# Weight sums of the first two column pairs of the first MLP product: added by transfers from GpSimd's queue in place of VectorE

## The chip, the core and the metric

The kernel runs on one core of a Trainium2 chip. The core has a matrix engine (TensorE, PE in the profile), VectorE (DVE), ScalarE (ACT), GpSimd (POOL) and SyncE (SP), each with an in-order queue of its own, and 16 DMA engines that move data between DRAM and the core's memory. SP, ScalarE and GpSimd issue transfers; those that add into their destination are issued from GpSimd in this kernel. The metric is the time of one execution in device microseconds (us); lower is better.

## What is computed

One layer of an encoder on a 1024 x 1024 input in float32: a normalisation, mLSTM heads and differential attention side by side, an output projection, and an MLP. The change touches the MLP alone:

```python
u = rms(x, norm2_g[l]).astype(dt) @ w_ff1[l]     # 1024 x 1024 by 1024 x 4096
u = jnp.square(jax.nn.relu(u))
x = x + (u @ w_ff2[l]).astype(dt)
```

## The kernel before

Every float32 matrix product is made from three matmuls: each operand is cut into a high part (`cut_hi`, a copy on ScalarE) and the low rest (`cut_lo`, a subtraction on VectorE), and high x high, high x low and low x high are added up.

**The first MLP product.** The 4096 columns of the weight are 32 tiles of 128 columns, taken in 16 pairs, c = 0 to 15. Of a pair, tile 2c is loaded into `raw_e[c]` and tile 2c+1 into `raw_o[c]`, each 128 partitions x 2 halves x 512. Call the halves e0, e1 and o0, o1: the upper and lower 512 rows of the weight. The input is likewise split into four quarters, by rows and by tokens. Each pair is then computed with seven block products in place of eight, in the manner of Strassen and Winograd. Each block product is a `product` of 12 matmuls (four steps of k, three matmuls each), and is numbered:

| product | weight operand | tile that holds its parts | right operand |
|---|---|---|---|
| 1 | e0 | `w_a(c)`, half 0 | `x1` |
| 2 | e1 | `w_a(c)`, half 1 | `x2` |
| 6 | e0 + o0 + o1 ("u") | `wb`, half 0 | `x6` |
| 5 | o0 + o1 (`sum_s`, half 1 of "e") | `we`, half 1 | `x5` |
| 7 | o0 + e0 (`sum_7`, half 0 of "e") | `we`, half 0 | `x7` |
| 3 | e1 + e0 + o0 + o1 ("3") | `wb`, half 1 | `x3` |
| 4 | o1 ("d") | `wd0` or `wd1` | `x4` |

In the trace the parts carry an h or l (`weh`, `wel`). The weight sums are made in place, by VectorE, in this order: "d" is cut from o1 first, since the next sum overwrites o1; `sum_s` turns o1 into o0 + o1; `sum_7` turns o0 into o0 + e0; `sum_u` turns e0 into e0 + o0 + o1; `sum_3` turns e1 into e1 + e0 + o0 + o1. Then "u", "e" and "3" are cut. "e" is cut in one operation over both halves of `raw_o`.

**What sets the order.** Products 1 and 2 of the first six pairs run first, while the right operands are still being made; their results go to DRAM and are read back later. For that, e0 and e1 of pairs 0 and 1 are loaded once for the first products and a second time (`load_e(c, True)`, tiles `re0b` and `re1b`) for the sums. Then come the other five products pair by pair: 6, 5, 7, 3, 4 of pair 0, the same of pair 1, and so on.

The order on every queue is written out by hand: `when(t, f, ...)` puts a piece of work into a table at a time t, counted in block products, and the table is issued in order of t. The times set only the order; what an engine really waits for are its operands. The dictionary `moved` shifts single entries. In these units the last of the first products runs at 11; products 6, 5, 7, 3 and 4 of pair 0 stand at 12 to 16, and those of pair 1 at 17 to 21. Around them:

- `load_e` (line 1808) and `load_o` (1815) are issued by SP. `raw_o` of pair 1 goes into a slot that is free when the first `x5l` has been made.
- Lines 2014, 2017, 2020 and 2023 are the four sums.
- The cuts are lines 1789 (ScalarE) and 1792 (VectorE).
- `diff` (2080) makes the sums of quarters of the input, `make_v`, `make_w`, `c22`, `c12` and `c21` (1955 to 1970) combine results, and `relu2` (1925 to 1928) squares and stores them.
- GpSimd has nothing in its queue between 613 us (the root of the second normalisation) and the adding transfers for the weights of the second MLP product, from 733 us on.

Of the kernel before, what the change touches and what calls it, by code (L numbers as in the profile page):

```python
# [13 lines left out]
ALU = mybir.AluOpType  # L14
# [8 lines left out]
HB = 512  # L23
# [117 lines left out]
def hybrid_block_kernel(ctx: ExitStack, tc: tile.TileContext, xT, xR, w_v, w_k, w_c, w_va, w_qg, w_o, w_1, w_2, w_2q, vec, rel, outT):  # L141
    nc = tc.nc
# [176 lines left out]
    with tc.tile_pool(reuse_waits="tile", name="ps0", bufs=1, space=PSUM) as ps0:  # L319
# [219 lines left out]
        for i in range(2):  # L539
            n, k = [f"n{2 * i}", f"n{2 * i + 1}"], [f"kr{2 * i}", f"kr{2 * i + 1}"]  # L540
# [212 lines left out]
    clock, table, made = [0.0], [], []  # L753

    def when(t, f, *args):
        heapq.heappush(table, (t + moved.get(len(made), 0.0), len(made), f, args))
        made.append(t)
# [986 lines left out]
    for n in range(KT):  # L1744
        t = A["HF"] + u * parts_at[n][0][0]
# [3 lines left out]
        t = A["HF"] + u * ends[n]  # L1749
# [38 lines left out]
    def cut_hi(dst, src, idx=slice(None)):  # L1788
        nc.scalar.activation(dst[0][idx], src, AF.Copy)  # L1789

    def cut_lo(dst, src, idx=slice(None)):
        nc.vector.tensor_tensor(dst[1][idx], src, dst[0][idx].bitcast(F32), op=ALU.subtract)  # L1792
# [11 lines left out]
    raw_e, raw_o = {}, {}  # L1804

    def load_e(c, again=False):
        raw_e[c] = mpool2.tile([P, 2, HB], F32, tag="re", name=f"re{c}{'b' if again else ''}", bufs=2)
        nc.sync.dma_start(raw_e[c].rearrange("p a b -> p (a b)"), w_1[2 * c])

    def load_o(c):  # L1810
        if c % 2 == 0:
            raw_o[c] = mpool2.tile([P, 2, HB], F32, tag="ro", name=f"ro{c}")
        else:
            raw_o[c] = ypool.tile([P, 2, HB], F32, tag="y0_0", name=f"ro{c}")
        nc.sync.dma_start(raw_o[c].rearrange("p a b -> p (a b)"), w_1[2 * c + 1])
# [21 lines left out]
    for j in range(4):  # L1837
        t = A["XN"] + j * A["XD"]
# [3 lines left out]
        t = A["WN"] + j * A["WD"]  # L1842
# [19 lines left out]
    table = []  # L1862
# [36 lines left out]
    for c in range(N_FIRST):  # L1899
        when(max(2 * c - 1, 0), ops[1], c)  # L1900
        ends_at[1, c] = max(2 * c, 1)
        t = min(2 * c + 2, 2 * N_FIRST - 1)
        when(t, ops[2], c)
        ends_at[2, c] = t + 1
    t = 2 * N_FIRST
# [79 lines left out]
    for c in range(N_PAIR):  # L1985
        e = {i: ends_at[i, c] + 0.01 for i in ops}
# [12 lines left out]
        d = c == N_PAIR - 1  # L1999
# [11 lines left out]


    def sum_s(c):
        nc.vector.tensor_tensor(raw_o[c][:, 1], raw_o[c][:, 0], raw_o[c][:, 1], op=add)

    def sum_7(c):
        nc.vector.tensor_tensor(raw_o[c][:, 0], raw_o[c][:, 0], raw_e[c][:, 0], op=add)

    def sum_u(c):
        nc.vector.tensor_tensor(raw_e[c][:, 0], raw_e[c][:, 0], raw_o[c][:, 1], op=add)  # L2020

    def sum_3(c):
        nc.vector.tensor_tensor(raw_e[c][:, 1], raw_e[c][:, 1], raw_e[c][:, 0], op=add)

    parts_of = {
# [7 lines left out]
    def when_cut(hi, lo, x, c):  # L2033
        when(hi, lambda: cut_hi(*parts_of[x](c)))
        when(lo, lambda: cut_lo(*parts_of[x](c)))
# [4 lines left out]
    for n in range(1, N_PAIR):  # L2040
        b = begin[n - 1]
        if n == 1:

            when_cut(b + 2.2, b + 2.5, "d", n)
            when(b + 2.5, sum_s, n)
            when(b + 2.6, sum_7, n)
            when(b + 3.1, sum_u, n)
            when_cut(b + 3.45, b + 4.3, "u", n)
            when(b + 4.4, sum_3, n)
            when_cut(b + 3.8, b + 5.35, "e", n)  # L2050
            when_cut(b + 5.4, b + 5.9, "3", n)
        elif n <= N_FIRST:
            when_cut(b + 0.9, b + 1.55, "d", n)
            when(b + 1.6, sum_s, n)
            when(b + 2.3, sum_7, n)
            when(b + 2.31, sum_u, n)
            when_cut(b + 2.55, b + 2.8, "u", n)
            when(b + 3.3, sum_3, n)
            when_cut(b + 2.9, b + 3.55, "e", n)
            when_cut(b + 4.02, b + 4.25, "3", n)  # L2060
        else:
            when_cut(b + 2.5, b + 3.3, "d", n)
            when(b + 3.35, sum_s, n)
            when(b + 4.3, sum_7, n)
            when(b + 4.35, sum_u, n)
            when(b + 4.4, sum_3, n)
            when_cut(b + 5.3, b + 5.6, "e", n)
            when_cut(b + 5.8, b + 6.2, "u", n)
            when_cut(b + 7.5, b + 8.1, "3", n)
        if n >= N_FIRST:  # L2070
            when_cut(b + 1.5, b + 2.1, "a", n)
        if n + 2 < N_PAIR:
            when(begin[n] + (0.95 if n == 1 else -0.4 if n <= N_FIRST else 1.2), load_e, n + 2, n + 2 < N_FIRST)
            when(begin[n] + (0.95 if n == 1 else -0.8), load_o, n + 2)
# [10 lines left out]
    for j, t in enumerate((2.4, 3.6, 4.1, 4.6)):  # L2085
        when(t, normed, 1, j)
    when(0.1, load_e, 4)
    when(0.2, load_o, 0)
    when_cut(3.0, 3.2, "a", 4)
    when(3.1, load_e, 5)  # L2090
# [8 lines left out]
    for j in range(2):  # L2099
        d = 0.45 * j  # L2100
# [11 lines left out]
    when(10.2, sum_7, 0)  # L2112
    when(10.3, sum_u, 0)
    when_cut(10.5, 10.9, "u", 0)
    when_cut(10.95, 11.8, "e", 0)
    when(12.3, sum_3, 0)
    when_cut(12.4, 12.7, "3", 0)
    when(12.2, load_o, 1)
    when(12.5, load_o, 2)
    when(13.2, load_e, 2, True)  # L2120

# [13 lines left out]
    step_at, t = [], T2  # L2135
# [26 lines left out]
        table.append(x)  # L2162

    copier[0] = nc.sync

    def pairs(first, each, what):
        for n, (copy, more) in enumerate(zip(*what)):
            for x, d in ((copy, -2.6), (more, 0)):
                table.append((first + each * n + d, 10**6 + len(table), x[0], x[1:]))
# [209 lines left out]
    for s, (i, p, x) in enumerate(steps):  # L2379
        t, e = step_at[s], step_at[s + 1]  # L2380
        b = step_at[s - 2] if s >= 2 else T2 - 1.65 + 0.8 * s
# [19 lines left out]
        if p and x == 1:  # L2401
# [5 lines left out]
            if p in (2, 6, 3, 4):  # L2407
# [3 lines left out]
                else:  # L2411
                    d, one = {2: (r00, True), 3: (r01, True), 4: (zv, False)}[i]
# [127 lines left out]
```

## Time and profile before

| | |
|---|---|
| time, median of three runs | 1216.43 us (1215.98 to 1216.46) |
| the profiled execution: its own time / its span | 1220.52 / 1218.7 us |
| granted clock of TensorE | 1.00 |
| TensorE busy | 1205.9 us |
| VectorE / ScalarE / GpSimd busy | 909.6 / 705.3 / 307.6 us |
| bytes moved, mean rate | 276.85 MB, 227 GB/s |
| the first MLP product | from 607 us |
| products 6, 5, 7, 3, 4 of pair 0 | from 641.77 us |
| products 6, 5, 7, 3, 4 of pair 1 | from 656.90 us |

How to read the rows: a row of the order of time has its start and its duration in us, the engine, the line of the kernel, the operation, destination <- sources, and in brackets the idle time before it with what ended it. A row of waits has the total, the number of waits and the longest. A row of a window has its length, the busy time of TensorE, its weight loads, VectorE, ScalarE and GpSimd (with their instructions), the granted clock, the mean busy share of the 16 DMA engines, and GB/s. DMA rows give the size and the median time from issue to landing. Matmuls overlap, so their durations (0.39) are longer than the distance of their starts.

### The profile page before, as it was taken

The numbers are of one execution on the slowest core, as the hardware profiler recorded it, in microseconds if no ns is written. First come the engines' busy times: TensorE is split into PE (matmuls) and PEld (weight loads), VectorE is DVE, ScalarE is ACT, GpSimd is POOL, SyncE is SP. The second block draws the span as 40 slices with busy tenths as digits, with TensorE's granted clock in tenths as the row PEclk, the third lists the DMA queues.
The fourth block names the chain that finished last, engine by engine and source line by source line (L and its number), as shares of the span: only waits on it lengthen the run. The fifth ranks groups of instructions, "written<-read, shape, count | busy, mean of one in ns | idle before, by whom it ended". The sixth has DMA issues, their size and how long they took to land.

```text
span 1218.7 us, 18707 instructions
## 1 busy us (share of the span) xinstructions
PE 1205.9 (99%) x6925; PEld 1038.0 (85%) x6925; DVE 909.6 (75%) x1274; ACT 705.3 (58%) x1213; POOL 307.6 (25%) x359
## 2 busy tenths in 40 slices
PE   9999999999999999999999999999999999999998
PEld 8889888888878888888887788888888999999997
DVE  7885578984276787773889886666657878888888
ACT  7685457676456686654465454444536556555553
POOL 1135323553354474432400001010101102012111
PEclk9999999999999999999999999999999999999999
DMA  9972565344476799827955769989889979979896
GB/s 283 225 259 106 197 146 134 95 145 142 128 243 197 248 312 273 267 90 265 247 171 178 241 235 254 289 251 287 247 281 318 317 261 278 318 194 310 209 262 183
DMA packets 121919, 276.85 MB, mean 227 GB/s; under 512 B 11360, under 2 KB 36704, under 8 KB 121312
## 3 DMA queue, kind: packets, MB, share of 16 engines
q1 hardware_dynamic: 84980, 181.64, 44.5%
q0 software_dynamic: 24896, 72.39, 26.7%
q10 hardware_dynamic: 11952, 21.63, 4.8%
q8 instruction: 54, 0.88, 0.3%
q14 instruction: 37, 0.30, 0.1%
HBM read 216.28 MB, written 91.85 MB: 253 GB/s over the span
## 4 chain that ended last, share of the span: by engine, by line
PE 78%; DMA 9%; DVE 6%; ACT 3%; issue 2%; POOL 1%; SPq 0%; ACTq 0%; DVEq 0%; POOLq 0%
PE m L1876 7%; PE m L1878 7%; PE m L1877 7%; PE pav L1460 4%; PE pva L1330 4%; PE z L2289 4%; PE pl L1420 4%; PE z L2288 4%; PE z L2287 4%; PE z L2270 3%; PE z L2268 3%; PE z L2269 3%; PE pw L263 3%; PE pw L265 2%; PE pw L264 2%
## 5 line engine op out<-in xcount | busy, mean ns | idle before, releaser
L184 POOL DMA_DIRECT2D s<-in_w_dram x32 | 27.0, 843 | 261.1 <-DMA s<-s 194.2
L1425 DVE CUSTOM_DVE_ANT_0 l<-pl,toe 128x1024 f32<-128x1024 f32 x64 | 76.3, 1221 | 16.8 <-PE pl L1420 15.8
L1925 ACT ACTIVATE sq<-sq 128x512 f32<-128x512 f32 x48 | 30.2, 630 | 83.4 <-DVE sq L1964 64.2
L1431 ACT ACTIVATE l<-l,sm 128x1024 f32<-128x1024 f32 x64 | 73.2, 1148 | 0.5 <-DVE sm L1425 0.5
L2231 POOL DMA_DIRECT2D zw<-in_w_2q_dram x24 | 22.7, 1042 | 192.4 <-DVE wa1l L1792 40.5
L1460 PEld LDWEIGHTS pav<-v,at 128*128 128x128 f32 x512 | 61.5, 191 | 3.4 <-issue 1.1
L1460 PE MATMUL pav<-v,at 128*128 128x128 f32 x512 | 62.7, 275 | 0.0
L2289 PE MATMUL z<-wbh,wa1l 128*128 128x256 f32 x208 | 59.1, 284 | 0.6 <-DVE wa1l L1792 0.5
L2288 PE MATMUL z<-wbl,wa1h 128*128 128x256 f32 x208 | 58.9, 283 | 0.0
L2287 PE MATMUL z<-wbh,wa1h 128*128 128x256 f32 x208 | 58.8, 283 | 0.0
L1420 PE MATMUL pl<-kk,q 64*128 64x512 f32 x384 | 54.8, 409 | 0.2 <-DVE sm L1425 0.2
L263 PE MATMUL pj_c<-hhi,w_c 128*128 128x512 f32 x128 | 53.4, 417 | 0.0
L263 PE MATMUL pw<-mix,hi_wo 128*128 128x512 f32 x128 | 52.0, 406 | 0.0
L265 PE MATMUL pj_c<-hhi,w_c 128*128 128x512 f32 x128 | 50.2, 392 | 0.0
L265 PE MATMUL pw<-mix,lo_wo 128*128 128x512 f32 x128 | 50.0, 391 | 0.0
L264 PE MATMUL pj_c<-hlo,w_c 128*128 128x512 f32 x128 | 50.0, 390 | 0.0
L264 PE MATMUL pw<-mix,hi_wo 128*128 128x512 f32 x128 | 49.9, 390 | 0.0
L2270 PE MATMUL z<-weh,wa0l 128*128 128x512 f32 x120 | 46.9, 391 | 1.5 <-DVE wa0l L1792 1.5
L2268 PE MATMUL z<-weh,wa0h 128*128 128x512 f32 x120 | 47.0, 391 | 0.7 <-ACT wa0h L1789 0.7
L2269 PE MATMUL z<-wel,wa0h 128*128 128x512 f32 x120 | 46.9, 391 | 0.0
L1420 PEld LDWEIGHTS pl<-kk,q 64*128 64x128 f32 x384 | 34.9, 184 | 12.2 <-issue 4.6
L1465 ACT ACTIVATE on<-pav 128x128 f32<-128x128 f32 x32 | 8.9, 277 | 60.5 <-PE pav L1460 60.5
(549 smaller groups left out, 4195.6 us busy)
## 6 DMA issues: line engine op xcount, KB each, us to landing
s<-in_w_dram POOLq DMA_DIRECT2D x40, 512.0 KB, 7.8
g_dram<-gs SPq DMA_DIRECT2D x64, 256.0 KB, 5.7
zw<-s SPq DMA_DIRECT2D x32, 512.0 KB, 9.9
g<-g_dram SPq DMA_DIRECT2D x24, 512.0 KB, 9.4
zw<-in_w_2q_dram SPq DMA_DIRECT2D x24, 512.0 KB, 6.6
zw<-in_w_2q_dram POOLq DMA_DIRECT2D x24, 512.0 KB, 9.3
wide<-g_dram SPq DMA_DIRECT2D x24, 512.0 KB, 12.3
g_dram<-sq ACTq DMA_DIRECT2D x42, 256.0 KB, 4.2
```

The lines of the kernel that those rows point to most:

```text
L263: nc.tensor.matmul(out, ahi, bhi, start=start, stop=False)
L264: nc.tensor.matmul(out, ahi, blo, start=False, stop=False)
L265: latest[0] = nc.tensor.matmul(out, alo, bhi, start=False, stop=stop).ins
L1420: nc.tensor.matmul(it.pl[x][:, sl], hd.q[r, i, qi * P : (qi + 1) * P], hd.kk[r, j, sl], start=n == 0, stop=n == 2)
L1460: nc.tensor.matmul(it.pav[:, 0:P], at, it.head.v[:, c], start=c == 0, stop=c == NC - 1)
L1876: nc.tensor.matmul(p, wh, xh, start=go, stop=False, skip_group_check=True)
L1877: nc.tensor.matmul(p, wh, xl, start=False, stop=False, skip_group_check=True)
L1878: nc.tensor.matmul(p, wl, xh, start=False, stop=stop and k == 3, skip_group_check=True)
L2268: nc.tensor.matmul(p, wh, gh, start=go, stop=False, skip_group_check=True)
L2287: nc.tensor.matmul(o, wh[:, j, nn], gh[:, j], start=go, stop=False, skip_group_check=True)
L2288: nc.tensor.matmul(o, wh[:, j, nn], gl[:, j], start=False, stop=False, skip_group_check=True)
L2289: nc.tensor.matmul(o, wl[:, j, nn], gh[:, j], start=False, stop=end, skip_group_check=True)
```

## The change

For pairs 0 and 1 the four sums are not made by VectorE. Each operand is made in place by transfers that read a half of a weight tile from DRAM and add it to a half of `raw_e` or `raw_o` in the core's memory: 256 KB each, issued by GpSimd. `sum_s` and `sum_7` become one such transfer each, at the places where the sums stood; `sum_u` and `sum_3` issue nothing; in their place stand five transfers a pair into `raw_e`, which add o0 and o1 to e0, and e0, o0 and o1 to e1. These have times of their own in the table. Three cuts or loads get other times: "d" of pair 1 earlier, "e" of pair 0 later, `load_o` of pair 1 a little earlier. Pairs 2 to 15 are as before.

```diff
+    def add_block(raw, c, half, n):
+        nc.gpsimd.dma_start(raw[c][:, half], w_1[2 * c + n // 2][:, n % 2 * HB : (n % 2 + 1) * HB], accum_op=ALU.add)
...
     def sum_s(c):
+        if c < 2:
+            return add_block(raw_o, c, 1, 2)
         nc.vector.tensor_tensor(raw_o[c][:, 1], raw_o[c][:, 0], raw_o[c][:, 1], op=add)
 
     def sum_7(c):
+        if c < 2:
+            return add_block(raw_o, c, 0, 0)
         nc.vector.tensor_tensor(raw_o[c][:, 0], raw_o[c][:, 0], raw_e[c][:, 0], op=add)
 
     def sum_u(c):
+        if c < 2:
+            return None
         nc.vector.tensor_tensor(raw_e[c][:, 0], raw_e[c][:, 0], raw_o[c][:, 1], op=add)
 
     def sum_3(c):
+        if c < 2:
+            return None
         nc.vector.tensor_tensor(raw_e[c][:, 1], raw_e[c][:, 1], raw_e[c][:, 0], op=add)
...
-            when_cut(b + 2.2, b + 2.5, "d", n)
+            when_cut(b + 1.9, b + 2.1, "d", n)
...
-    when_cut(10.95, 11.8, "e", 0)
+    when_cut(12.0, 12.3, "e", 0)
...
-    when(12.2, load_o, 1)
+    when(11.95, load_o, 1)
...
     copier[0] = nc.sync
+    for t, c, adds in ((5.3, 0, ((0, 2), (1, 0))), (6.9, 0, ((0, 3), (1, 2))), (9.0, 0, ((1, 3),)), (9.01, 1, ((0, 2), (1, 0))),
+                       (10.9, 1, ((0, 3), (1, 2))), (12.2, 1, ((1, 3),))):
+        for half, n in adds:
+            table.append((t, 10**6 + len(table), add_block, (raw_e, c, half, n)))
```

In `add_block` n counts the four blocks of a pair: 0 and 1 are e0 and e1, 2 and 3 are o0 and o1.

## The prediction

> **What bounds the kernel now.** First the page's line of engines, then what TensorE waited for around the change, then TensorE's own order of time there.
>
> ```profile
> span 1218.7 us, 18707 instructions
> PE 1205.9 (99%) x6925; PEld 1038.0 (85%) x6925; DVE 909.6 (75%) x1274; ACT 705.3 (58%) x1213; POOL 307.6 (25%) x359
> ```
>
> TensorE is the bound: 99% of the span. Anything taken off another engine can give back only what TensorE waits for it. The waits of TensorE between 600 and 700 us:
>
> ```profile
> PE m L1876 <- ACT wbh L1789: 0.6, 1, 0.6
> PE m L1877 <- DVE x4l L1792: 0.4, 1, 0.4
> PE m L1876 <- DVE sq L1964: 0.3, 1, 0.3
> PE m L1876 <- DVE w L1959: 0.2, 1, 0.2
> ```
>
> Each is a wait of a few tenths, 1.5 us in all. Now TensorE itself: the first matmuls of products 6 and 5 of pair 0, the one of product 5 that first reads the low part `wel`, the two late ones, and the first matmul of product 5 of pair 1.
>
> ```profile
> 641.77 0.39 PE L1876 MATMUL m<-x6h,wbh 128*128 128x512 f32 x1
> 644.49 0.39 PE L1876 MATMUL m<-x5h,weh 128*128 128x512 f32 x1
> 644.95 0.39 PE L1878 MATMUL m<-x5h,wel 128*128 128x512 f32 x1
> ...
> 654.86 0.50 PE L1877 MATMUL m<-x4l,wd0h 128*128 128x512 f32 x1 [0.44 <-DVE x4l L1792]
> 656.90 0.50 PE L1876 MATMUL m<-x6h,wbh 128*128 128x512 f32 x1 [0.62 <-ACT wbh L1789]
> 660.02 0.39 PE L1876 MATMUL m<-x5h,weh 128*128 128x512 f32 x1
> ```
>
> A product of 12 matmuls takes 644.49 - 641.77 = 2.72 us, 0.227 a matmul. From 641.77 to 660.02 lie six products, which would take 16.33; they took 18.25. So 1.92 us is all that this stretch can give. With the later waits of 0.3 and 0.2 it is 2.4: about 0.2% of 1216.43, which is also about what a measurement of this kernel can tell from no change. Gain is capped; loss is not.
>
> **The change, part by part.** VectorE around it, and ScalarE's high part of `we`:
>
> ```profile
> 635.25 0.68 DVE L1792 TENSOR_TENSOR wd0l<-ro,wd0h 128x512 fp32r<-128x512 f32 x1
> 635.96 0.69 DVE L2014 TENSOR_TENSOR ro<-ro 128x512 f32<-128x512 f32 x1
> 636.69 0.69 DVE L2017 TENSOR_TENSOR ro<-ro,re0b 128x512 f32<-128x512 f32 x1
> 637.42 0.69 DVE L2020 TENSOR_TENSOR re0b<-re0b,ro 128x512 f32<-128x512 f32 x1
> ...
> 640.90 1.22 DVE L1792 TENSOR_TENSOR x5l<-y,x5h 128x1024 fp32r<-128x1024 f32 x1
> 642.04 1.21 DVE L1792 TENSOR_TENSOR wel<-ro,weh 128x1024 fp32r<-128x1024 f32 x1
> 643.17 0.68 DVE L2023 TENSOR_TENSOR re0b<-re0b 128x512 f32<-128x512 f32 x1
> 643.78 2.35 DVE L1792 TENSOR_TENSOR x7l<-y,x7h 128x1024 fp32r<-128x1024 f32 x2
> ```
>
> ```profile
> 639.49 1.05 ACT L1789 ACTIVATE weh<-ro 128x1024 fp32r<-128x1024 f32 x1
> ```
>
> Removed: four sums of 0.69 for each of two pairs, 5.5 us of a VectorE that is full there. Worth at most the 1.92.
>
> Added: seven adding transfers of 256 KB a pair, all on GpSimd's in-order queue. By the times in the table of work they stand there so: A1 (e0+=o0), A2 (e1+=e0), A3 (e0+=o1), A4 (e1+=o0), A5 (e1+=o1), then A6 and A7, the first two of pair 1; only then A8 (`sum_s`: o1+=o0) and A9 (`sum_7`: o0+=e0) of pair 0; then the rest of pair 1. A1 needs `re0b`; A3 needs A1 landed, A4 needs A2, A5 needs A4. That a transfer into a tile waits on GpSimd for the one before to land, the first row below shows. Each such wait holds up everything behind it, A8 and A9 too.
>
> What does an add cost? The trace has no such chain, but at 1188 us one 512 KB add is followed by four of 256 KB into halves of tiles, nothing else moving (times to landing are counted from issue):
>
> ```profile
> 1023.57 0.86 POOL L2231 DMA_DIRECT2D zw<-in_w_2q_dram  x1 [7.50 <-DMA zw<-in_w_2q_dram]
> ...
> 1187.99 0.85 POOL L2231 DMA_DIRECT2D zw<-in_w_2q_dram  x1 [3.83 <-DVE wa1l L1792]
> zw<-in_w_2q_dram POOLq DMA_DIRECT2D x1, 512.0 KB, 5.4
> L2298 POOL DMA_DIRECT2D ra<-y_dram x4: 1187/1688/2190, 1188.5 to 1190.2; - x4
> DMA to landing us min/median/max: 6.9/8.0/9.1
> 1193.50:1194.00 0.50, 0.50 (x3) 0.39 (x3) 0.47 (x1) 0.00 (x0) 0.00 (x0) 1.00 1.13 201
> ```
>
> The first 256 KB landed at 1188.5 + 6.9 = 1195.4, the fourth at 1190.2 + 9.1 = 1199.3: 1.3 us each, and the last row says why (DMA share 1.13 at 201 GB/s: adds fill all engines at that rate). A lone add of 256 KB, L, is then 5.4 - 1.3 = 4.1 us; the ends are 3.6 (the plain 512 KB load below) and 5.4 (no saving for the half size).
>
> [...]
>
> When does the chain start? `re0b` is issued and loads like it land so:
>
> ```profile
> 621.25 0.38 SPq L1808 DMA_DIRECT2D re0b<-in_w_dram  x1
> ro<-in_w_dram SPq DMA_DIRECT2D x2, 512.0 KB, 3.6
> re<-in_w_dram SPq DMA_DIRECT2D x16, 512.0 KB, 5.5
> ```
>
> With 4.0 (the engines are half busy then, see below) it lands at 625.3. A2, second in line, lands at 625.3 + 4.1 + 1.3 = 630.7; A4 4.1 later, 634.8; A5 is issued then. A6 to A9 are right behind it: `re1b` has come by about 633, and `wd0l`, which A8 must wait for, ends at 635.9. Five adds in a row: A9 lands 4.1 + 4 x 1.3 = 9.3 later, at **644.1**, if nothing else moves; in general at 625.3 + 3L + 6.5. But something does (DMA share and GB/s last):
>
> ```profile
> 625.00:637.00 12.00, 12.00 (x54) 9.95 (x53) 11.93 (x13) 10.18 (x14) 0.00 (x0) 1.00 0.51 176
> 637.00:644.00 7.00, 7.00 (x32) 5.82 (x31) 6.97 (x9) 5.99 (x10) 0.00 (x0) 1.00 0.41 147
> ```
>
> From 637 to 644 the other queues keep the engines busy 0.41 x 7 = 2.9 us, and five adds need 6.5: together more than fits, so the adds, last in line, pay up to the 2.9. From 627 to 635 others take about 4 of 8 us and four adds 5.2: up to 1.2 more. So with L = 4.1 A9 lands between 644.1 and 648.2, and between 642.6 and 652.1 with the ends of L; I take **647.0**: 2.9 of the 4.1, since the last in line meets the later load for certain.
>
> Moved: `cut` of "e" comes later in the order of ScalarE and VectorE. It reads both halves of `ro`, so it waits for A9: `weh` 647.05 to 648.1, `wel` 648.15 to 649.35. TensorE wants `wel` at 644.95: **4.45 us of stall**. Queued behind `weh` on ScalarE are the last of the first products' squares and the cuts of "3" and "d"; behind `wel` on VectorE are both `x7l` and all that follows. At trace durations (starts of full-width operations 1.14 apart, half-width 0.6): `x7l` to 651.6, `v` 652.2, `y` 653.4, `w` 654.0, `wd1l` 654.6, `wbl` of "3" 655.2. TensorE would want that `wbl` at 649.4 + 10 x 0.227 + 2.72 + 0.45 = 654.85: 0.4 more. Then `x4l` to 656.35, `y` 657.5, `x4h` on ScalarE 658.6, second `x4l` 659.85, wanted at 659.1: 0.8 more. Product 5 of pair 1 so starts at 663.8, not 660.02: **+3.8 us**. In other words 4.45 of stall, less the 0.65 of old waits that vanish in it.
>
> The smaller edits: `load_o` of pair 1 passes nothing on SP's queue (nothing of SP's lies between its two times) and still waits for the first `x5l`: nothing, and at worst a part of the 2.9 above. The earlier "d" of pair 1 lets A13 and A14 go sooner; they have about 9 us from `wd1l` to the use of `weh`, and need 4.1 + 1.3 + the cuts 2.4 = 7.8: nothing, up to 1 us late under load. The new transfers add 3.7 MB, which no load that TensorE waits for meets but these.
>
> **The sum.** 1216.43 + 3.8 = 1220.2; the profiled execution, 1220.52 by its own clock, 4.1 above the median of the three runs, would show 1224.3. The late case by itself reaches from A9 at 645.6 (+2.4) to 648.2 (+5.0): 1218.9 to 1221.4.
>
> **Rivals.**
> 1. *The adds are in time* (not slower). If L is under 3.8 and the other queues give way, A9 lands before 643.1, and no stall counts. VectorE, 5.5 us lighter, then has the first `x4l` at 651.0 (after `w`, which as now waits for a store until 648.0), `y` 652.1, `x4h` 653.2, the second `x4l` 654.5, wanted at 654.2; the `wbh` wait goes. Of the 1.92 about 0.4 stays: -1.5, 1214.9. For it: the half-empty queues; against it: the three landings in a row and A6, A7 ahead of A8. A little late, A9 between 643.1 and 645.6, is 0 to +2.4. The deciding point is A9 at 645.6: later is slower by over 0.2%.
> 2. *The clock.*
>
> ```profile
> PEclk9999999999999999999999999999999999999999
> ...
> PE z L2270 <- DVE zwl L1792: 1.2, 1, 1.2
> ```
>
>    TensorE would stand still from the end of product 6, about 644.6, to 648.1: 3.5 us, where its longest wait from 641 us to the end is 1.2. If the granted clock, full in every slice, halved for one product after it, that is 2.7 us more: 1222.9. For it speaks only that no wait of this length is in the trace; against it that the clock never falls. [...]
> 3. *Faster*: every wait up to 700 us vanishes and nothing is late: -2.4, 1214.0. Against it: the chain of `x4h` stands whatever VectorE sums.
> 4. *It doesn't reach the path*: VectorE's sums were hidden and the adds are too: 1216.4. Speaks for it that only 1.92 us are to be had.
>
> **How the numbers follow.** Late by over 0.2%: 0.55, and with the clock 0.08; in time 0.20, a little late 0.09, not on the path 0.05, faster 0.03. So slower 0.63, same 0.34, faster 0.03. The range takes in the in-time case's -1.5 and, above, A9 at 648.2 with part of the clock's price: 1214.6 (a little below its middle) to 1222.6.
>
> **What would show it.** In the profile after: no VectorE row of L2014 to L2023 before 662 us; A9's landing about 647; one wait of TensorE in product 5 for `weh` or `wel`, 3 to 5 us long, with ScalarE's `weh` put down to the adding transfer; GpSimd idle before A3, A4 and A5 behind landings; SP's second `ro` load, which waits for `wel`, 6 us later; the granted clock at 1.00 or not. The prediction is wrong if A9 lands by 643, if adds of half a tile run faster than 201 GB/s, or if the stall is there and pair 1's products catch up more than 0.65.

## The result, and the profile after

The changed kernel takes **1227.0 us** (median of five runs, 1225.39 to 1229.37) against 1216.43 (five runs beside it, 1215.98 to 1216.93): ratio 1.0084, 95% interval 1.0073 to 1.0094. It is slower by 10.6 us; forecast were 3.8, with 1222.6 as the upper end. The profiled execution of the changed kernel is the fastest of its five (1225.39), that of the kernel before was 4.1 above its median, so their spans differ by 4.9 only.

The page's engines of the kernel after, then TensorE's waits between 600 and 760 us (total, number, longest):

```profile
span 1223.6 us, 18728 instructions
PE 1207.1 (99%) x6925; PEld 1039.6 (85%) x6925; DVE 904.8 (74%) x1266; ACT 705.7 (58%) x1213; POOL 321.4 (26%) x373
```

```profile
PE m L1879 <- ACT weh L1789: 7.2, 1, 7.2
PE m L1881 <- DVE wel L1792: 0.4, 1, 0.4
PE m L1879 <- DVE sq L1967: 0.3, 1, 0.3
```

The eight sums have left VectorE (1274 to 1266 instructions), the fourteen transfers stand on GpSimd (359 to 373), and in place of four waits of a few tenths there is one of 7.2 us, for `weh`, with two of a few tenths behind it. TensorE's, ScalarE's and VectorE's order of time there, then GpSimd's (start, duration, and in brackets the idle time before with its releaser; "x2" are two issues in one row):

```profile
641.73 0.39 PE L1879 MATMUL m<-x6h,wbh 128*128 128x512 f32 x1
...
651.81 0.79 PE L1879 MATMUL m<-x5h,weh 128*128 128x512 f32 x1 [7.20 <-ACT weh L1789]
...
656.69 0.40 PE L1879 MATMUL m<-x7h,weh 128*128 128x512 f32 x1
...
664.90 0.39 PE L1879 MATMUL m<-x6h,wbh 128*128 128x512 f32 x1
...
667.69 0.39 PE L1879 MATMUL m<-x5h,weh 128*128 128x512 f32 x1
...
668.71 0.50 PE L1881 MATMUL m<-x5h,wel 128*128 128x512 f32 x1 [0.41 <-DVE wel L1792]
```

```profile
650.70 1.06 ACT L1789 ACTIVATE weh<-ro 128x1024 fp32r<-128x1024 f32 x1 [9.61 <-DMA ro<-in_w_dram]
```

```profile
651.79 1.23 DVE L1792 TENSOR_TENSOR wel<-ro,weh 128x1024 fp32r<-128x1024 f32 x1 [9.99 <-ACT weh L1789]
```

```profile
625.53 1.82 POOL L1811 DMA_DIRECT2D re0b<-in_w_dram  x2 [12.35 <-DVE wa1l L1792]
630.07 0.85 POOL L1811 DMA_DIRECT2D re0b<-in_w_dram  x1 [2.72 <-DMA re0b<-in_w_dram]
633.99 0.88 POOL L1811 DMA_DIRECT2D re0b<-in_w_dram  x1 [3.06 <-DMA re0b<-in_w_dram]
640.02 0.86 POOL L1811 DMA_DIRECT2D re0b<-in_w_dram  x1 [5.15 <-DMA re0b<-in_w_dram]
640.68 1.95 POOL L1811 DMA_DIRECT2D re1b<-in_w_dram  x2
641.76 2.64 POOL L1811 DMA_DIRECT2D ro<-in_w_dram  x2
```

Read it backwards: TensorE waits for `weh`, ScalarE's `weh` for the add into `ro` (A9, landed 650.7), and A8 and A9 were issued from 641.8 us on, behind A5, which waited 5.15 us on GpSimd for A4 to land. A1 and A2 go at 625.5, A3 at 630.1, A4 at 634.0, A5 at 640.0.

The transfers between 625 and 651 us, by queue (packets, MB, share of the time of 16 engines), first before, then after; q0 carries GpSimd's transfers, q1 SP's and q10 ScalarE's. Behind each the row of windows (the last two numbers are DMA share and GB/s):

```profile
q1 hardware_dynamic: 1178, 2.99, 38.2%
q10 hardware_dynamic: 720, 1.31, 13.3%
```

```profile
625.00:651.00 26.00, 26.00 (x116) 21.55 (x115) 25.57 (x28) 18.27 (x25) 0.00 (x0) 1.00 0.52 166
```

```profile
q0 software_dynamic: 1383, 2.54, 58.0%
q1 hardware_dynamic: 864, 2.10, 23.7%
q10 hardware_dynamic: 576, 1.05, 11.3%
```

```profile
625.00:651.00 26.00, 19.61 (x87) 15.91 (x85) 15.08 (x14) 14.31 (x20) 9.65 (x11) 0.96 0.93 219
```

The engines, half idle before (share 0.52), are nearly full after (0.93). The adds take 0.580 x 26 = 15.1 us for 2.54 MB, 5.9 us a MB, or 1.56 us for one of 256 KB (262,144 bytes); the other queues take (23.7 + 11.3)% of 26 = 9.1 us for 3.15 MB, 2.9 us a MB. In this stretch a byte that is added costs twice the engine time of a byte that is moved.

**Where the 10.6 us are.** From the first matmul of product 6 of pair 0 to the first of the second MLP product:

```profile
916.78 0.39 PE L2268 MATMUL z<-weh,wa0h 128*128 128x512 f32 x1
```

```profile
924.94 0.39 PE L2283 MATMUL z<-weh,wa0h 128*128 128x512 f32 x1
```

916.78 - 641.77 = 275.01 before, 924.94 - 641.73 = 283.21 after: 8.2 us, 8.0 of them lost by product 6 of pair 1 (15.13 us after that of pair 0 before, 23.17 after). The other 2.4 of the medians' difference is in no trace: four of the five runs after are 0.4 to 4.0 us above the profiled one. The stretch from product 6 to the second product is used below to compare single executions, as it leaves out what they differ by elsewhere.

### The profile page after: what moved, and what is told of

Same layout as the page of the kernel before. It is cut to its first block, busy times and chain, and to the rows that moved or that the text cites. A ratio compares the mean times of both kernels' runs of the same rounds, so it can differ in the third digit from the quotient of the medians.

```text
span 1223.6 us, 18728 instructions
## 1 busy us (share of the span) xinstructions
PE 1207.1 (99%) x6925; PEld 1039.6 (85%) x6925; DVE 904.8 (74%) x1266; ACT 705.7 (58%) x1213; POOL 321.4 (26%) x373
## 5 line engine op out<-in xcount | busy, mean ns | idle before, releaser
L2246 POOL DMA_DIRECT2D zw<-in_w_2q_dram x24 | 22.5, 1013 | 189.6 <-DVE wa1l L1792 72.0
L1792 DVE TENSOR_TENSOR wel<-ro,weh 128x1024 fp32r<-128x1024 f32 x16 | 19.6, 1223 | 36.2 <-ACT weh L1789 36.2
```

## The experiments

| run | median, us | ratio (95% interval) | longest wait of TensorE there | product 6 to second product |
|---|---|---|---|---|
| before | 1216.43 | | 0.6 | 275.0 |
| after | 1227.00 | 1.0084 (1.0073 to 1.0094) | 7.2 | 283.2 |
| pair0_only | 1224.72 | 1.0067 (1.0055 to 1.0079) | 4.6 | 281.8 |
| pair1_only | 1218.77 | 1.0019 (1.0009 to 1.0028) | 0.6 | 276.6 |
| o_first | 1222.16 | 1.0046 (1.0034 to 1.0058) | 3.3 | 278.3 |
| pair0_o_first | 1219.24 | 1.0017 (1.0008 to 1.0026) | 0.6 | 276.5 |
| swap | 1226.95 | 1.0081 (1.0065 to 1.0097) | 7.2 | 284.0 |
| load_later | 1225.67 | 1.0071 (1.0057 to 1.0085) | 6.3 | 283.7 |
| filler | 1227.84 | 1.0095 (1.0080 to 1.0111) | 3.1 | 284.7 |
| filler_long | 1229.25 | 1.0094 (1.0077 to 1.0111) | 0.4 | 283.5 |
| no_sums | 1214.29 | 0.9977 (0.9968 to 0.9987) | 0.2 | 272.5 |
| two_adds | 1219.48 | 1.0019 (1.0010 to 1.0028) | 0.6 | 275.7 |
| sum3_only | 1219.55 | 1.0022 (1.0013 to 1.0030) | 2.4 | 277.4 |

Each ratio is against the kernel before on the same chip (1216.4 to 1216.7). The edits are against the changed kernel; in them `adds` stands for its list of added rows, "..." for code left out, and a condition that stands in several sums is shown once.

### Which adds make A9 late: pair 0's, pair 1's, their order

**Pair 0 alone.** Pair 1 is summed on VectorE as before, so A6 and A7 are gone from ahead of A8; of `adds` the five rows of pair 0 stay.

```diff
-        if c < 2:
+        if c < 1:
...
-            when_cut(b + 1.9, b + 2.1, "d", n)
+            when_cut(b + 2.2, b + 2.5, "d", n)
```

> Only pair 0 is made by adding transfers; pair 1's sums are VectorE's again. Queue theory (A9 is late because it stands behind A5's wait and then behind the data of A6 and A7): A9 lands two transfers, 2.6 us, sooner, about 648.0; TensorE's wait for weh falls from 7.2 to about 4.6, and the time from 1227.0 to about 1224.5. Rival (the waits inside pair 0 set everything, pair 1's adds are beside the point): the wait stays at 7 us and the time at 1226 to 1227.

Measured: 1224.72, a wait of 4.6, `weh` at 648.65; A9 landed 22.5 us after the first add was issued instead of 25.2. Two adds fewer ahead of A9 brought it 2.7 us forward, a little less than 2 x 1.56. That is as the theory of a queue had it, in the wait and in the time. More than half of the loss comes from pair 0's own adds.

**Pair 1 alone.** The opposite: pair 0 as before, "e" at its old times; of `adds` the five rows of pair 1 stay.

```diff
-        if c < 2:
+        if c == 1:
...
-    when_cut(12.0, 12.3, "e", 0)
+    when_cut(10.95, 11.8, "e", 0)
```

> Only pair 1 is made by adding transfers; pair 0's sums are VectorE's, with the cut of e at its old times. Queue theory: no long wait at pair 0's product 5; the clock stays at 1.00; pair 1's last two adds may make weh up to 1.3 us late: 1215.5 to 1217.7. Rival (the adds cost by loading the DMA engines, wherever they stand): about half of the loss remains, 1221 or more, with waits spread over several products.

Measured: 1218.77, above the range of the one theory and below the rival's, and no wait is over 0.6. ScalarE's "d" of pair 1 shows what the adds do to a neighbour:

```profile
646.42 0.63 ACT L1789 ACTIVATE wd1h<-ro 128x512 fp32r<-128x512 f32 x1 [2.45 <-DMA ro<-in_w_dram]
```

It waits 2.45 us for the plain load of `ro`, which took 6.5 us beside pair 1's first adds (from the first `x5l`, made at 639.8; 3.6 before), and the rest of ScalarE's queue stands behind it. VectorE is lighter by four sums here and nothing is gained.

**Another order.** A9 goes third instead of last, A8 ahead of pair 1's adds; all fourteen stay.

```diff
     def sum_7(c):
         if c < 2:
-            return add_block(raw_o, c, 0, 0)
+            return None
...
-    adds
+        (5.3, raw_e, 0, 0, 2), (5.3, raw_e, 0, 1, 0), (5.31, raw_o, 0, 0, 0), (6.9, raw_e, 0, 0, 3), (6.9, raw_e, 0, 1, 2),
+        (10.21, raw_e, 1, 0, 2), (10.21, raw_e, 1, 1, 0), (10.3, raw_e, 0, 1, 3), (10.9, raw_e, 1, 0, 3),
+        (10.9, raw_e, 1, 1, 2), (12.0, raw_o, 1, 0, 0), (12.2, raw_e, 1, 1, 3),
```

> All fourteen adds, in another order: o0+=e0 of pair 0 third in the queue, o1+=o0 of pair 0 ahead of A5, A6 and A7, and the same for pair 1 as far as its loads allow. The same bytes, the same sums off VectorE. Queue theory: the last add of weh of pair 0 is issued at about 636 and lands at 641 to 642, the wait for weh falls to 0 to 1 us, the clock stays full, and the time comes to 1215 to 1217.5. Rival (14 adds are too much for the DMA engines here): a wait of 3 us or more stays, 1221 or more.

Measured: 1222.16. The wait at product 5 is gone, as expected; the time is the rival's. The first row is VectorE's, the second TensorE's:

```profile
653.22 0.69 DVE L1962 TENSOR_TENSOR w<-v,m 128x512 f32<-128x512 f32 x1 [1.88 <-DMA g_dram<-w_s]
```

```profile
654.05 0.76 PE L1879 MATMUL m<-x3h,wbh 128*128 128x512 f32 x1 [3.34 <-DVE w L1962]
```

A store of 256 KB that ScalarE had issued at 644.91 landed at 653.2, 8.3 us later, and `w` overwrites what it reads; product 3 waits for `w`. The same 3.7 MB still go through full engines (share 1.07 from 645 to 653 us): with A8 and A9 early, something else is late. Still, the order alone took 4.8 us off the changed kernel's time.

**That order, pair 0 only.** Pair 1 on VectorE; "e" of pair 0 after the last square.

```diff
-        if c < 2:
+        if c < 1:
...
-            return add_block(raw_o, c, 0, 0)
+            return None
...
-            when_cut(b + 1.9, b + 2.1, "d", n)
+            when_cut(b + 2.2, b + 2.5, "d", n)
...
-    when_cut(12.0, 12.3, "e", 0)
+    when_cut(12.02, 12.3, "e", 0)
...
-    adds
+        (5.3, raw_e, 0, 0, 2), (5.3, raw_e, 0, 1, 0), (5.31, raw_o, 0, 0, 0), (6.9, raw_e, 0, 0, 3),
+        (6.9, raw_e, 0, 1, 2), (10.3, raw_e, 0, 1, 3),
```

> Only pair 0 by adding transfers, in the order of o_first (o0+=e0 third, o1+=o0 ahead of A5), pair 1 by VectorE, and ScalarE squares the last first product ahead of the cut of e. Seven adds less than o_first lie on the DMA engines from 637 to 655 us. Theory (what was left in o_first, 3.3 us before product 3, came from the store of w_s that took 8 us among pair 1's adds): no wait over 1 us at products 5, 7, 3; the clock stays full; 1215.0 to 1217. Rival (A5 alone, waiting for A4, makes the operand of product 3 late): a wait of 2 us or more before product 3, 1219 or more.

Measured: 1219.24, slower than before by 0.08 to 0.26%, with a full clock and no long wait: the rival's time without the rival's wait, so neither expectation came. VectorE in two windows (its busy time is the third number after the window's length):

```profile
640.00:646.00 6.00, 5.85 (x25) 4.54 (x26) 2.14 (x3) 4.64 (x7) 0.85 (x1) 1.00 1.04 284
646.00:652.00 6.00, 5.47 (x24) 4.19 (x24) 6.00 (x7) 2.20 (x3) 0.00 (x0) 1.00 0.52 167
```

It is busy for 2.14 us of the first six, behind a `wel` that waits for `weh` (ScalarE makes it at 644.60, after the last square; at 639.49 before), and for all of the next six; in the kernel before it is busy for 6.00 and 5.67. So the time that was freed lies where VectorE had nothing to do yet.

### Chain or bytes

**Swap.** A2 is issued ahead of A1 and A4 ahead of A3, so the chain A2, A4, A5 is an add shorter, with the same bytes.

```diff
-... ((5.3, 0, ((0, 2), (1, 0))), (6.9, 0, ((0, 3), (1, 2))), ...
+... ((5.3, 0, ((1, 0), (0, 2))), (6.9, 0, ((1, 2), (0, 3))), ...
```

> The changed kernel with A2 issued ahead of A1 and A4 ahead of A3: the same bytes, the same engines, but the chain A2, A4, A5 that holds the queue no longer stands second each time. Chain theory: A5 is issued at about 637.6, where it was at 640.0, A9 lands 2.4 sooner, and the wait for weh falls from 7.2 to about 4.8; time about 1224.5. Rival (the DMA engines are full from 631 us on and A9 lands when all bytes are through): the wait stays between 6.5 and 7.5, 1226 to 1227.5.

```profile
626.74 1.82 POOL L1811 DMA_DIRECT2D re0b<-in_w_dram  x2 [12.45 <-DVE wa1l L1792]
...
638.34 0.86 POOL L1811 DMA_DIRECT2D re0b<-in_w_dram  x1 [3.51 <-DMA re0b<-in_w_dram]
```

```profile
651.84 1.06 ACT L1789 ACTIVATE weh<-ro 128x1024 fp32r<-128x1024 f32 x1 [9.39 <-DMA ro<-in_w_dram]
```

A5 is issued 638.34 - 626.74 = 11.6 us after the first add, 2.9 sooner than after (14.5). A9 still lands 25.1 us after the first add (25.2), and the wait is 7.24. The waits on GpSimd's queue, which the prediction counted one by one, did not set the end. The theory of the chain falls, and the rival's forecast, that A9 lands when the bytes are through, came: the engines' share until A9 landed was 0.95 after and 0.98 in swap.

**A load moved.** As pair0_only, with `re1b`'s 512 KB loaded at 638.9 in place of 628.7 us.

```diff
-    when(7.0, load_e, 1, True)
+    when(12.1, load_e, 1, True)
```

> pair0_only with the second load of e0 and e1 of pair 1, 512 KB, issued after the load of o0 and o1 of pair 1 in place of 628 us: this traffic no longer meets A2, A3 and A4. Contention theory (a load ahead of an add holds it up by its own 1.4 us and more): A4 is issued 1.5 to 2.5 sooner than at 633.3, A9 lands 1.5 to 2.5 sooner than 648.6, the wait falls from 4.6 to 2 to 3, time 1222.5 or less. Rival (an add takes 6 us or more by itself in such a chain): A9's landing and the wait stay within 0.7.

Measured: 1225.67 and a wait of 6.3, more than pair0_only's 4.6; A4 and A5 went 0.25 and 1.3 us sooner, counted from the first add, but A9 landed 24.2 us after it (22.5). Neither expectation came: the wait grew. Until A9 landed the same bytes were moved in both kernels, 1.84 MB of adds and 3.15 MB of others. By the shares of the queues they kept the engines busy for 20.0 us in pair0_only and 21.3 in load_later, and left them 2.5 and 2.9 us of gaps. So gaps, as from 636 to 638 us (share 0.65, 1.07 in pair0_only), where the next add waits for a landing, explain at most 0.4 of the 1.7 us. The rest is that the same bytes held the engines 1.3 us longer where the load met A5 to A9; why is not shown.

**Two adds alone.** Of pair 0 only A8 and A9 are made; its other two sums are left out, so products 6, 1, 2 and 3 read raw blocks.

```diff
-        if c < 2:
+        if c < 1:
...
-            when_cut(b + 1.9, b + 2.1, "d", n)
+            when_cut(b + 2.2, b + 2.5, "d", n)
...
-    adds
```

> Of pair 0 only A8 and A9 are made (as adding transfers, "e" at its late time); its other two sums are left out (the operands of products 6, 1, 2 and 3 read raw blocks). Pair 1 as before, summed on VectorE. So 0.5 MB of adds instead of 3.5, nothing ahead of them on GpSimd's queue. If the bytes of the seven other adds, with the loads, are what made A9 late: A8 and A9 are issued at about 636, land by 642 to 643, no wait at product 5 and a clock of 1.00, 1215.5 to 1217.0. Rival, an adding transfer is slow among loads and stores whatever stands ahead of it (7 us each, as A3 and A4 were): A9 lands at 645 to 650, a wait of 2 to 6 us, 1219 to 1224.

The issue on GpSimd, `weh` on ScalarE, and the adds' row in the view of transfers (count, KB, median us to landing):

```profile
636.12 1.82 POOL L1811 DMA_DIRECT2D ro<-in_w_dram  x2 [23.26 <-DVE wd0l L1792]
```

```profile
643.10 1.06 ACT L1789 ACTIVATE weh<-ro 128x1024 fp32r<-128x1024 f32 x1 [2.74 <-DMA ro<-in_w_dram]
```

```profile
ro<-in_w_dram POOLq DMA_DIRECT2D x2, 256.0 KB, 5.2
```

With nothing ahead of them they land by 643.1, `wel` is 0.5 us late and the clock stays at 1.00: A9's lateness comes from the seven other adds ahead of it. The profiled execution took 1217.17, just above the range expected; it is the fastest of eleven, and the median, 1219.48, lies in the rival's range. So even this version with 0.5 MB of adds costs some 3 us, of which the trace shows 0.7; the rest is open.

### What is to be had, and a smaller version

**No sums at all.** The weight sums of both pairs are left out; the products read raw blocks.

```diff
-            return add_block(raw_o, c, 1, 2)
+            return None
...
-            return add_block(raw_o, c, 0, 0)
+            return None
...
-            when_cut(b + 1.9, b + 2.1, "d", n)
+            when_cut(b + 2.2, b + 2.5, "d", n)
...
-    when_cut(12.0, 12.3, "e", 0)
+    when_cut(10.95, 11.8, "e", 0)
...
-    adds
```

> Leaves out the weight sums of pairs 0 and 1 altogether (no VectorE sums, no adding transfers; the products read raw blocks); cuts of "e" and "d" at their old times, the load of the second o at its new one. It shows the most that freeing VectorE of these sums could give. Theory, as the in-time rival of the prediction had it: of the 1.92 us of waits around products 4 and 6 about 1.5 goes, 1214.9 (1214.0 to 1215.5), and the waits for x4l and wbh shrink. Rival, from pair0_o_first and pair1_only, where VectorE was lighter and nothing was gained: the freed time stands behind other waits (stores, PSUM banks, squares), 1216.0 to 1216.8, and waits of a few tenths stay.

Measured: 1214.29, 0.13 to 0.32% faster. First matmuls of product 6 of pair 0, of product 5 of pair 1 and of the second MLP product:

```profile
640.93 0.39 PE L1879 MATMUL m<-x6h,wbh 128*128 128x512 f32 x1
...
657.25 0.39 PE L1879 MATMUL m<-x5h,weh 128*128 128x512 f32 x1
...
913.43 0.39 PE L2278 MATMUL z<-weh,wa0h 128*128 128x512 f32 x1
```

The first two are 16.32 us apart, six products without a wait: the 1.92 of the forecast's cap are real. To the second product it is 272.5 us, 2.5 less than before, and this is about all that the change could win. So VectorE's sums do cost something here, and the rival, that nothing was to be had, falls.

**Only the sum of "3".** A2, A4 and A5 of each pair, 1.6 MB of adds in all and none ahead of `weh`. Against the kernel before, only `sum_3` of the two pairs and these rows are changed.

```diff
-    adds
+        (5.3, raw_e, 0, 1, 0), (6.9, raw_e, 0, 1, 2), (9.0, raw_e, 0, 1, 3),
+        (9.01, raw_e, 1, 1, 0), (10.9, raw_e, 1, 1, 2), (12.2, raw_e, 1, 1, 3),
```

> Only the sum of "3" of each of the two pairs is made by transfers (A2, A4, A5: three adds of 256 KB into one half tile, landed in a row); the other three sums stay on VectorE at their old times, "e" and "d" too. 1.5 MB of adds in place of 3.5, and none of them ahead of weh: the operand is wanted at about 650, 25 us after the tile is loaded. A version that might beat both kernels: the sums replaced are one VectorE operation of 0.69 a pair. If nothing else is disturbed: 1215.5 to 1216.6, no wait over 1 us, clock 1.00. Rival, the adds slow the loads and stores beside them (as in o_first and pair1_only): 1217 to 1219, with waits behind DMA landings.

Measured: 1219.55; the rival's wait came, and the time is a little above its range. VectorE's `w` again:

```profile
651.22 0.69 DVE L1962 TENSOR_TENSOR w<-v,m 128x512 f32<-128x512 f32 x1 [4.00 <-DMA g_dram<-w_s]
```

The store issued at 643.01 landed at 651.2, and product 3 waited 2.4 us. None of the versions that make sums by transfers beat the kernel before.

### What the slow clock cost

TensorE's clock by windows after (granted clock, then DMA share and GB/s):

```profile
650.00:652.00 2.00, 0.19 (x1) 0.20 (x2) 0.21 (x1) 1.30 (x2) 0.00 (x0) 0.50 1.00 165
652.00:654.00 2.00, 1.96 (x4) 1.14 (x5) 2.00 (x2) 1.53 (x4) 0.00 (x0) 0.50 0.59 125
654.00:656.00 2.00, 2.00 (x7) 1.52 (x5) 2.00 (x4) 0.49 (x1) 0.86 (x1) 0.57 0.98 304
656.00:658.00 2.00, 2.00 (x10) 1.66 (x9) 2.00 (x3) 0.95 (x1) 0.00 (x0) 1.00 1.05 247
```

Product 5 ran at half clock for most of its length: 656.69 - 651.81 = 4.88 us for 2.72. Is that in the loss? Extra matmuls of which nobody reads the result keep TensorE at work during the wait:

```diff
+    def filler():
+        p = psF.tile([P, HB], F32, tag="q3", name="filler")
+        for _ in range(2):
+            product(p, wb, at(0), 6, True, True)
+
+    table.append((12.5, 10**6 + len(table), filler, ()))
```

> The changed kernel with 24 matmuls more between products 6 and 5 of pair 0, into a bank that nobody reads: TensorE works 5.4 of the 7.2 us in which it stood still. Clock theory (the stall costs a slow clock on top, about 1.9 us): the clock is 1.00 in product 5, which then takes 2.7 and not 4.9 us, and the time falls by about 1.9, to 1225. Rival (product 5 is slow for its operands): no change, 1227.

The 24 matmuls were too few: A9 landed later in this run (652.0), a wait of 3.06 us was left, and the clock fell all the same (0.50 from 654 to 657 us, product 5 from 653.12 to 658.14). So it doesn't tell the two theories apart; it only shows a fall behind a wait of 3.06 us. With `range(3)`, 36 matmuls:

> The changed kernel with 36 idle-time matmuls in place of 24: TensorE works until about 652.5, past the landing of A9 at 650.6 to 652. Clock theory (any wait of 3 us or more drops the clock, as the 3.06 us did that the 24 matmuls left): the clock is 1.00 all through product 5, which takes 2.7 to 3.0 us in place of 4.9; product 7 then starts at about 655.5 in place of 656.7, and the time is 0 to 1.5 below that of the change. Rival (the slow clock comes from the DMA load or the adds, not from the wait): product 5 is slow again, product 7 starts at 657.5 or later.

```profile
652.41 0.39 PE L1879 MATMUL m<-x5h,weh 128*128 128x512 f32 x1
...
655.40 0.39 PE L1879 MATMUL m<-x7h,weh 128*128 128x512 f32 x1
...
661.77 0.47 PE L1879 MATMUL m<-x4h,wd0h 128*128 128x512 f32 x1 [0.40 <-DVE sq L1967]
```

Now the clock is 1.00 throughout and product 5 takes 2.99. Product 7 begins at 655.40, 1.29 us before that of the changed kernel (656.69). But product 6 of pair 1 begins at 664.70, only 0.20 before 664.90, and the stretch to the second product is 283.5 against 283.2. The gain is lost again in products 3 and 4, where TensorE waits for VectorE (the last row): `wel` begins at 651.73 and 651.79 in the two kernels, and VectorE's work behind it takes as long in both (that `sq` begins at 660.94 and 661.03). So in these two executions the slow product is hidden behind VectorE. The lower time that the clock theory had did not come: the median, 1229.25, is 3.6 above the profiled execution, and no trace shows why.

## Why the prediction was right and wrong

**Right: the direction, and the path from A9 to TensorE.** `cut` of "e" waits for A9, TensorE for `weh`, and GpSimd stands before A3, A4 and A5 behind landings. The cap of 1.92 is confirmed by no_sums (16.32 us for the six products; the first rival's price was -1.5, and -2.2 were measured), so slower was the likely side.

**Wrong: when A9 lands.** That is the step that failed: 647.0 was taken, 644.1 to 648.2 the bounds for L = 4.1, 650.7 was measured. The lone add was sized well: the first add of pair 0 landed 3.7 (sum3_only) to 4.3 us (in the changed kernel) after its issue. What was too small is the term for the load of the other queues: up to 4.1 us in all, of which 2.9 were taken, for the last five adds alone. Under that load A2 landed 7.5 us after its issue (5.4 forecast) and A4 5.7 (4.1); so A4 was issued at 634.0 (630.7 forecast), A5 at 640.0 (634.8), and the last part took 10.7 (12.2). The prediction's outer bound for L = 5.4, 652.1, holds the measured landing, but its stated range stopped at 648.2 and a part of the clock's price. With A9 at 650.7 its own sum would have been 3.8 + 3.7 = 7.5, or 1223.9.

Swap shows why no repair of a single wait would do: shortening the chain by 2.9 us left A9 where it was. What binds is the engine time of what stands ahead of A9 and beside it. The prediction had both terms for such a sum: nine adds of 1.3 are 11.7 us, and the other queues' 0.52 of the 26 us from 625 to 651 are 13.5; from 625.5 they end at 650.7. That this meets the landing to the tenth is luck, and the 0.52 is read off a window that is known only afterwards: after, the terms were about 9 x 1.56 = 14.0 and 9.1, since some loads slid behind the stall, with about two us of gaps and of the adds behind A9. (The 1.3 were measured at a share of 1.13, so they were 1.47 of engine time.) Latency and load were treated as things that overlap unless they are seen to collide; with engines as full as here (a share of 0.95 until A9 landed) they did not.

The first rival, with the adds in time, wanted an L under 3.8. From issue to landing the shortest add of a weight block took 3.7 (sum3_only), the two of two_adds 5.2 in the median, and in the changed kernel, beside the other queues, the medians are 5.7 (`re0b`) and 8.0 (A8 and A9); that rival did not come.

**The chain behind `wel` was right.** Predicted: from `wel` at 648.15 to product 5 of pair 1 at 663.8, 15.65 us. Measured: 667.69 - 651.79 = 15.9. So of the 7.67 us by which that product is later than before, 3.8 were forecast, 3.64 are A9's lateness and 0.25 the chain. As a sum by TensorE's own waits it is: first matmul of product 5 of pair 0 later by 7.32, plus 2.16 for its half clock, less 1.81 of old waits that went. The forecast's 0.65 regained was too small as such, since the VectorE work behind `wel`, now without sums, is what sets the pace; for the same reason the 2.16 is hardly an extra loss.

**The clock.** The second rival was given 0.08 and 2.7 us. No row of the kernel before shows a clock that falls; the halving was the author's assumption. After, the granted clock was 0.50 from 649 to 655.5 us, and product 5 took 2.16 more. But filler_long, with a full clock, is no sooner at product 6 of pair 1: its cost here is about nothing. The forecast counted on a clock that stays full and was wrong in that; that leaving out the clock's price did no harm was luck, since nobody had seen that VectorE would hide it.

**The smaller edits.** The earlier "d" of pair 1 was priced at nothing, up to 1 us late: `wel` of pair 1 was 0.4 late, within the bound. That the new bytes meet no load that TensorE waits for holds for the changed kernel up to 700 us, but not in general: o_first and sum3_only lost time to a slow store (8.3 and 8.2 us, 4.8 before), and in pair1_only a plain load was slow (6.5, 3.6 before).

**What stays open.** 2.4 of the 10.6 us, the difference between the medians and what the traces show from product 6 to the second product; and likewise 2.3 and 3.6 us in two_adds and filler_long, whose profiled executions were the fastest of theirs. Which later wait does it was not seen; the kernel before scatters too (its profiled execution is 4.1 above its median).

## What to carry to other kernels

Before moving arithmetic into adding transfers, add up the engine time in the window in which they must land: the share that other queues have there, plus each add at its measured price (1.56 us for 256 KB here, twice that of a plain transfer). If the sum is near the window, don't count on a shorter chain of waits: in swap 2.9 us less of it left the landing where it was (25.1 us after the first add, 25.2 without), and in o_first another order made a store late (8.3 us) in place of an operand. First measure what the freed engine is worth by leaving the work out: here it was 0.2%. And when a wait is added, look for the engine whose queue stands behind it: in filler_long its remaining work, not TensorE's own speed, said when the loss ends (product 7 began 1.29 us sooner, product 6 of pair 1 only 0.20).

## What the hardware showed that was not expected

**The clock's raster.** The granted clock fell after waits of 2.39 us (sum3_only), 3.06 (filler), 3.34 (o_first), 4.6 and more, and not after the 1.2 of the kernel before. The fall came 2.0 (o_first, load_later) to 4.7 us (swap) after TensorE's last matmul, in filler and sum3_only when it was at work again. Windows of half a microsecond in which the clock changes, for three kernels (sum3_only, after, load_later; the granted clock is the third number from the end):

```profile
652.00:652.50 0.50, 0.44 (x1) 0.45 (x2) 0.50 (x2) 0.00 (x0) 0.00 (x0) 0.62 0.36 29
655.50:656.00 0.50, 0.50 (x3) 0.38 (x2) 0.48 (x1) 0.50 (x2) 0.00 (x0) 0.97 0.99 373
```

```profile
648.50:649.00 0.50, 0.00 (x0) 0.00 (x0) 0.00 (x0) 0.00 (x0) 0.50 (x1) 0.90 1.11 201
655.50:656.00 0.50, 0.50 (x4) 0.39 (x2) 0.50 (x2) 0.00 (x0) 0.00 (x0) 0.77 1.01 410
```

```profile
646.00:646.50 0.50, 0.00 (x0) 0.00 (x0) 0.00 (x0) 0.00 (x0) 0.00 (x0) 0.61 1.06 283
656.00:656.50 0.50, 0.50 (x3) 0.37 (x2) 0.12 (x1) 0.50 (x1) 0.00 (x0) 0.65 0.00 0
```

A mean of 0.62 over half a microsecond is 0.12 us at full and 0.38 at half clock (0.50 in the windows between), so the first slow stretch runs from 652.12 to 655.53, 3.41 us; the second from 648.90 to 655.73, 6.83; the third from 646.11 to 656.35, 10.24: one, two and three times 3.41. Read in the same way, the slow stretches of filler (3.42), pair0_only (6.83), o_first (6.83) and swap (6.82) fit too: in these seven traces the clock changed at edges 3.41 us apart. By the same reading the 3.41 us before the fall had TensorE idle for 58% in o_first, 59% in load_later, 70% in sum3_only, 79% in filler, and throughout in after, swap and pair0_only. If the edges lie at this distance ahead of the fall too, the 3.41 us before those were idle for 26% (after) and 37% (swap), and no fall followed them.

**Stores beside adds landed late.** From the issue of a plain store of 256 KB to the start of `w`, which waits for it, it was 8.3 us in o_first and 8.2 in sum3_only; before, the same store was issued at 643.43 and took 4.8:

```profile
648.19 0.69 DVE L1959 TENSOR_TENSOR w<-v,m 128x512 f32<-128x512 f32 x1 [0.33 <-DMA g_dram<-w_s]
```

In o_first the engines were full all the while. In sum3_only the share was 0.92 from 643 to 649 us, but 0.10 in the last two us, so full engines don't explain these; what the store waited for then is not shown:

```profile
649.00:651.00 2.00, 0.67 (x3) 0.21 (x2) 0.00 (x0) 0.00 (x0) 0.11 (x1) 1.00 0.10 36
```

While the stalled kernel had only adds to move (646 to 652 us), the engines, at a share of 1.09, brought 186 GB/s.

```profile
646.00:652.00 6.00, 0.19 (x1) 0.20 (x2) 0.21 (x1) 1.30 (x2) 1.71 (x2) 0.74 1.09 186
```
